# A hybrid delta-rule layer: projections ranked last, operations moved between in-order queues, and the sample states' product in 64 scaled copies on ScalarE

## Chip, cores, metric

The kernel runs on one core of a Trainium2 chip. The metric is the device time of one execution in microseconds (us): the median of several runs, and for the reading of where the time lies one profiled execution. The engines of the core are PE (matmuls; its weight loads are listed apart as PEld), DVE (VectorE), ACT (ScalarE), POOL (GpSimd) and SP (which here only issues transfers). Each works through its own instructions in order.

## What is computed

One layer of a decoder for a prompt of 1024 tokens and for eight samples of one token each, all in float32, with 1024 model columns, 8 delta heads of 128 and a feed-forward width of 2816:

```python
h = _rmsnorm(x, lp['norm1_w']) * (1 + sc1) + sh1
qkv, gdn_gate, beta_raw, a_raw, sq, sk, sv, ga, gb = _split_in(h @ lp['w_in'])
...
if st is None:
    o_a, S = _gdn_chunked(q, k, v, beta, g)              # prompt: chunks of 64
else:
    o_a, S = _gdn_recurrent(q, k, v, beta, g, st['gdn_S'])   # samples: one step
y_a = _gdn_out(o_a, gdn_gate, lp['gdn_onorm_w']) @ lp['w_gdn_out']
y_b = o_b @ lp['w_swa_out']                              # o_b: sliding-window attention with sinks
mix = (jax.nn.sigmoid(ga) * y_a + jax.nn.sigmoid(gb) * y_b) @ lp['w_o']
x = x + gt1 * mix
h2 = _rmsnorm(x, lp['norm2_w']) * (1 + sc2) + sh2
gate = h2 @ lp['w_ffn_gate']
up = h2 @ lp['w_ffn_up']
gc = _causal_dwconv(gate_ext, lp['ffn_conv_w'], L) + lp['ffn_conv_b']    # 3 taps
x = x + gt2 * ((jax.nn.silu(gc) * up) @ lp['w_ffn_down'])
```

The state of a sample's head is updated as `S = S * exp(g) + k ⊗ delta`, a 128x128 matrix for each of 64 pairs of sample and head; it is an output.

## The kernel before

Every product is made of three matmuls (L178, L179, L180 in `mm3`): both operands are split into a high part (`hi`, a ScalarE copy with rounding, L127) and the rest (`lo`, a VectorE subtraction, L128), and hi·hi, lo·hi and hi·lo are added in PSUM. So each weight tile takes a load on SP's queue (`raw`), a split on ScalarE and one on VectorE before PE can use it. Where a tile has one buffer, the next load waits for the split of the last, and the split waits for the last matmul that reads the one before.

The work goes by stages. By the times of the profile below they are: setup, modulation and attention (0 to 437 us), the delta heads (437 to 1153), the branches' output projections (1153 to 1330), the projection with w_o and the second norm (1330 to 1436), the FFN's gate and up products (1436 to 1886), its down product (to 2086) and the last chain of it with the final norm (to 2134.5).

The order of instructions on each engine is fixed when the program is built, by a scheduler that simulates the timeline and takes, among what could go next, what has the lowest priority number. `weave` sets these numbers for several streams of a delta head: each has a start and a step, and its operations get start, start + step, and so on. `unit_inverse` (start 0, step 1) inverts a head's triangular blocks: transposes and small products on PE (L1028, L1034, L1046, L1051, L1060, L1064), each followed by copies on ScalarE (L1030, L1048, L1053, L1055, L1061) or VectorE (L1035, L1057), with two rounds through DRAM on SP's queue: blocks are stored and reloaded in another layout (L987 and L992; L1015 and L1018). `delta_scan` (100, 1) walks the head's chunks (L937 to L966), `delta_prepare` makes the next head's operands, and `head_projections` the products with w_in for the head after next. `pieces` are the fillers: the products for the branch gates (`gates`, which ends in a tanh on ScalarE, L1284, an operation on GpSimd, L1285, and a store on SP, L1286) and for part of w_swa_out (`early_out`, L1306 and L1310); they start at 10000. The fillers' weights have one buffer until the head before the last.

`branches` multiplies the two branches by w_swa_out and w_gdn_out and gates them; `gate_part` loads the stored gates (L1376). Between its products `sample_delta` updates the samples' states: for each head the delta rows are loaded spread over all partitions (L1204, two buffers), GpSimd multiplies the 128x1024 tile by the keys (L1205), and VectorE adds it to the decayed state in eight operations (L1207).

`ffn_gate_up` makes the convolution in three VectorE operations per tile, of which the first (L1662) scales and adds the bias. `pair_weights` makes sums and differences of weight tiles (L1572) for a form with fewer products; they are on GpSimd except for the first tile, which is given to VectorE. `ffn_down` runs 77 steps of three matmuls on eight PSUM banks; `fetch` loads, adds and splits a step's operands some 13 steps ahead, and `take` (L1766) copies the banks out on ScalarE at the end of a chain.

## Time and profile before

| | |
|---|---|
| Time | 2136.81 us median of 3 runs (2132.54 to 2142.25) |
| Profiled execution | 2136.28 us, span 2134.5 us |
| Mean granted TensorE clock | 0.979 |
| PE busy | 2046.5 us (96%) |
| DVE, ACT, POOL busy | 1393.5 us (65%), 854.7 us (40%), 534.6 us (25%) |

A row of the stage table gives the stretch in us, its length, then busy time and (count) for PE, PEld, DVE, ACT and POOL, the mean granted clock of TensorE, the share of time that the DMA engines were busy, and GB/s. A row of a table of waits names the waiting engine, tile and line, what ended the wait, and total, times and longest in us. A row of the timeline gives start, duration, engine and operation, and in brackets the idle time ahead of it and what ended it. A row of a table of groups ends in busy us and mean ns of one, and the idle time ahead of the group. A row that gives three numbers with slashes has the minimum, median and maximum ns of one operation. "DMA b1l<-dlr: 23.1, 6" below such a row says that the engine was idle ahead of it for 23.1 us, six times, until that transfer; a row that begins with POOL there is read in the same way.

### The profile page before, as it was taken

The page shows a single profiled execution, that of the slowest core. Times are in us where ns is not written, and L with a number is a line of the kernel's source. Part 1 is how long each engine was busy: PE and PEld are TensorE (multiplying, and loading weights), DVE is VectorE, ACT ScalarE, POOL GpSimd, SP SyncE. Part 2 cuts the span into 40 slices and gives each one's busy share as a digit, 9 for nine tenths or more (in the row PEclk, how much of TensorE's full clock was granted, in tenths as well). Part 3 has the DMA queues.
Part 4 walks back from the last instruction along what each step waited for, and adds up shares of the span by engine and source line. Part 5 has one row for each costly group of instructions (what it writes and reads, how often), then busy time and mean ns, then how long its engine had stood idle before and what let it go on. Part 6 is the DMA issues. An engine that isn't in the chain of part 4 may idle for free. (4 is left out here: it accounts for less than half of the span.)

```text
span 2134.5 us, 41210 instructions
## 1 busy us (share of the span) xinstructions
PE 2046.5 (96%) x16245; PEld 1935.3 (91%) x16245; DVE 1393.5 (65%) x2781; ACT 854.7 (40%) x2125; POOL 534.6 (25%) x592
## 2 busy tenths in 40 slices
PE   7999999999899999999989989998999999999898
PEld 4985888899899999999879989898999999999898
DVE  4756667465655736557445575479888788678866
ACT  3655445434244233443343222344343343343443
POOL 1000000020221211212110220003546546545531
PEclk8999999999999999999989999999999999999999
DMA  7256442141332322313166663622333333388972
GB/s 272 86 133 204 141 161 90 49 135 48 76 85 58 83 58 54 89 52 76 48 183 211 213 224 100 182 61 71 109 95 95 110 95 95 120 285 276 317 228 85
DMA packets 301821, 274.95 MB, mean 129 GB/s; under 512 B 59666, under 2 KB 248303, under 8 KB 301612
## 3 DMA queue, kind: packets, MB, share of 16 engines
q1 hardware_dynamic: 296140, 252.49, 38.6%
q0 software_dynamic: 5200, 19.32, 2.6%
q8 instruction: 127, 2.08, 0.4%
q14 instruction: 66, 0.54, 0.1%
q10 hardware_dynamic: 288, 0.52, 0.1%
HBM read 212.54 MB, written 62.12 MB: 129 GB/s over the span
## 5 line engine op out<-in xcount | busy, mean ns | idle before, releaser
L178 PE MATMUL mm<-b1h,wh 128*128 128x384 f32 (+1 forms) x1520 | 499.0, 329 | 5.9 <-ACT gt L1284 4.1
L180 PE MATMUL mm<-b1h,wl 128*128 128x384 f32 (+1 forms) x1520 | 491.4, 325 | 2.1 <-DVE wl L128 2.1
L179 PE MATMUL mm<-b1l,wh 128*128 128x384 f32 (+1 forms) x1520 | 490.8, 323 | 0.0
L178 PEld LDWEIGHTS mm<-b1h,wh 128*128 128x128 f32 x1520 | 287.8, 190 | 15.7 <-ACT gt L1284 6.2
L180 PEld LDWEIGHTS mm<-b1h,wl 128*128 128x128 f32 x1520 | 287.3, 189 | 7.9 <-issue 4.3
L179 PEld LDWEIGHTS mm<-b1l,wh 128*128 128x128 f32 x1520 | 288.0, 189 | 3.8 <-issue 3.5
L127 ACT ACTIVATE wh<-raw 128x1024 fp32r<-128x1024 f32 x83 | 87.0, 1048 | 135.7 <-PE mm L179 75.9
L128 DVE TENSOR_TENSOR wl<-raw,wh 128x1024 fp32r<-128x1024 f32 x82 | 100.8, 1229 | 48.8 <-ACT wh L127 47.9
L179 PE MATMUL mm<-pk,w 128*128 128x260 f32 (+1 forms) x440 | 124.3, 283 | 1.1 <-DVE pk L128 1.1
L178 PE MATMUL mm<-pk,w 128*128 128x260 f32 (+1 forms) x440 | 124.3, 283 | 0.0
L180 PE MATMUL mm<-pk,w 128*128 128x260 f32 (+1 forms) x440 | 124.2, 282 | 0.0
L128 DVE TENSOR_TENSOR w<-ws,w 128x512 fp32r<-128x512 f32 x88 | 74.1, 843 | 37.4 <-ACT w L127 37.4
L1609 ACT COPY bml<-mm 128x256 f32<-128x256 f32 (+1 forms) x132 | 49.2, 374 | 108.5 <-PE mm L180 101.8
L178 PE MATMUL mm<-bmh,w 128*128 128x260 f32 (+1 forms) x320 | 90.4, 283 | 0.9 <-DVE fa L1686 0.9
L180 PE MATMUL mm<-bmh,w 128*128 128x260 f32 (+1 forms) x320 | 90.3, 282 | 0.0
L180 PE MATMUL mm<-b2h,wl 128*128 128x384 f32 (+1 forms) x256 | 83.4, 329 | 4.5 <-DVE wl L128 4.5
L178 PE MATMUL mm<-b2h,wh 128*128 128x384 f32 (+1 forms) x256 | 83.8, 329 | 2.4 <-DVE t L1327 2.4
L179 PE MATMUL mm<-b2l,wh 128*128 128x384 f32 (+1 forms) x256 | 83.9, 328 | 0.4 <-DVE b2l L128 0.4
L179 PEld LDWEIGHTS mm<-pk,w 128*128 128x128 f32 x440 | 82.8, 188 | 1.3 <-DVE pk L128 1.3
L178 PEld LDWEIGHTS mm<-pk,w 128*128 128x128 f32 x440 | 82.8, 188 | 0.3 <-ACT bml L1609 0.2
L180 PEld LDWEIGHTS mm<-pk,w 128*128 128x128 f32 x440 | 83.0, 189 | 0.0
L127 ACT ACTIVATE w<-ws 128x512 fp32r<-128x512 f32 x88 | 55.4, 632 | 49.9 <-PE wv L180 45.0
(648 smaller groups left out, 5984.1 us busy)
## 6 DMA issues: line engine op xcount, KB each, us to landing
raw<-in_w_in_dram SPq DMA_DIRECT2D x60, 512.0 KB
ws<-in_w_ffn_down_dram SPq DMA_DIRECT2D x55, 256.0 KB
raw<-xd SPq DMA_DIRECT2D x47, 258.0 KB
raw<-in_w_ffn_down_dram SPq DMA_DIRECT2D x47, 256.0 KB
raw<-in_w_ffn_gate_dram SPq DMA_DIRECT2D x22, 512.0 KB
raw<-in_w_ffn_up_dram SPq DMA_DIRECT2D x22, 512.0 KB
qst<-in_w_mod_dram SPq DMA_DIRECT2D x16, 512.0 KB
raw<-in_w_mod_dram SPq DMA_DIRECT2D x16, 512.0 KB
```

Of the source, the lines that this page charges most:

```text
L127: self.nc.scalar.activation(hi, x, AF.Copy)
L128: (eng or self.nc.vector).tensor_tensor(lo, x, hi.bitcast(F32), op=ALU.subtract)
L178: mm(ps, whi, xhi, start=first, stop=False, **kw)
L179: mm(ps, whi, xlo, start=False, stop=False, **kw)
L180: self.last_mm = mm(ps, wlo, xhi, start=False, stop=last, **kw).ins
L1609: self.last_copy = nc.scalar.copy(r[p, i], x[p])
```

## The change

Eight edits. In `weave`, the streams whose operations set the priority at which the next call begins are now those with step 1, not those with a start under 10000; the streams of projections start at 100000, behind the fillers at 10000. In `sample_delta`, ScalarE multiplies by the keys, in eight copies of 128x128 per head (L1206 of the changed kernel), in place of GpSimd. `early_out` loads part 0 of the attention's output in its fourth step. The gates that `gate_part` loads into the extra pool go through GpSimd's queue. The first tap of the FFN convolution is on ScalarE. In `ffn_down`, the splits of later steps may not be ordered ahead of the last `take`, and the last two steps of a chain fetch nothing. The second half's `ffn_states` starts at 460, the first gate weights' sums go to GpSimd, and the PSUM banks of the branches begin with another one.

```diff
@@ -1202,8 +1202,8 @@
                 yield
             d = db[:, h % 2 * NP:h % 2 * NP + NP].rearrange("p (b v) -> p b v", b=NS)
             nc.sync.dma_start(d, dlr[h].unsqueeze(0).broadcast_to([P, NS, P]))
-            nc.gpsimd.tensor_tensor(d, d, bc(kq[:, h, :, 0], 2, P), op=ALU.mult)
             for b in range(NS):
+                nc.scalar.activation(d[:, b, :], d[:, b, :], AF.Copy, scale=kq[:, h, b, 0:1])
                 nc.vector.scalar_tensor_tensor(S0[h][:, b, :], S0[h][:, b, :], self.egb[:, b, 0, h:h + 1], d[:, b, :],
                                                op0=ALU.mult, op1=ALU.add)
             nc.gpsimd.dma_start(self.O[3][0][:, h].rearrange("b k v -> k b v"), S0[h])
@@ -1252,11 +1252,11 @@
         for gen, start, step in streams:
             at = tc.cur_priority = p + start
             for _ in gen:
-                if start < 10000:
+                if step == 1:
                     end = max(end, tc.cur_priority)
                 at += step
                 tc.cur_priority = max(at, tc.cur_priority) if step == 1 else at
-            if start < 10000:
+            if step == 1:
                 end = max(end, tc.cur_priority)
         tc.cur_priority = end
 
@@ -1300,7 +1300,6 @@
         self.S0, states = [], [self.flat_room(self.b1, "b1", x, 1) for x in "hl"]
         X = {2: self.load_part(self.b1, self.ob, 2, "b1")}
         w = load(0)
-        self.obX = {0: self.load_part(self.b1, self.ob, 0, "b1")}
         for j in range(8):
             s = self.t(self.gt[0], [P, 384], self.gt[1])[:, :n]
             nc.sync.dma_start(s, self.sgb[j][:, lo:lo + n])
@@ -1309,6 +1308,8 @@
                 nc.vector.tensor_tensor(s, ps, s, op=ALU.mult)
                 nc.sync.dma_start(self.ubd[j], s)
 
+            if j == 3:
+                self.obX = {0: self.load_part(self.b1, self.ob, 0, "b1")}
             now, w = w, load(j + 1) if j < 7 else None
             if j < 6:
                 self.load_state(j, states[j // 3])
@@ -1373,7 +1374,7 @@
 
     def gate_part(self, pool, src, t):
         s = (self.t(pool, [P, 384], "gt") if pool is self.gt[0] else self.t(pool, [P, 384], "sgx", bufs=2))[:, :PARTS[t][1]]
-        self.nc.sync.dma_start(s, src)
+        (self.nc.sync if pool is self.gt[0] else self.nc.gpsimd).dma_start(s, src)
         return s
 
 
@@ -1659,7 +1660,7 @@
             e = min(c + n, NP)
             zi, ai = z[i], a[i]
             col = lambda j: fcw[:, j, f + i:f + i + 1]
-            nc.vector.tensor_scalar(ai[:, c:e], zi[:, 2 + c:2 + e], col(2), col(3), op0=ALU.mult, op1=ALU.add)
+            nc.scalar.activation(ai[:, c:e], zi[:, 2 + c:2 + e], AF.Identity, scale=col(2), bias=col(3))
             for j in (0, 1):
                 nc.vector.scalar_tensor_tensor(ai[:, c:e], zi[:, j + c:j + e], col(j), ai[:, c:e],
                                                op0=ALU.mult, op1=ALU.add)
@@ -1719,6 +1720,7 @@
                 1: ((0, 0, 1), (1, 1, 1)), 2: ((0, 1, 1), (1, 1, -1)), 6: ((1, 1, 1),)}
         steps = [(i, g) for c in chains for i in c for g in range(G)]
         ready, waiting = {}, ([], [])
+        self.took = None
         less = []
 
         def fetch(s):
@@ -1739,9 +1741,8 @@
             room = self.room(tags[s % len(tags)], [P, KC * QW])
             hi, lo = room[:, :n + 512], room[:, n + 512:2 * (n + 512)]
             with ExitStack() as after:
-                if 5 <= s < len(tags):
-                    for ins in (self.last_up, self.last_copy):
-                        after.enter_context(self.tc.issue_after(ins.ins))
+                for ins in (self.last_up, self.last_copy) if 5 <= s < len(tags) else (self.took,) if s >= len(tags) and self.took else ():
+                    after.enter_context(self.tc.issue_after(ins.ins))
                 self.split(hi, lo, raw)
             ready[s] = hi, lo
             if s == 5:
@@ -1763,20 +1764,26 @@
         def take(ps, i, p, j):
             self.turn = (self.turn + 1) % KC
             r = self.copies[:, self.turn, :256 + 4 * p]
-            nc.scalar.copy(r, ps)
+            self.took = nc.scalar.copy(r, ps)
             for k, h in enumerate(home[i]):
                 waiting[k].append((r, p, j, *h))
 
         banks = [(self.pmm, "mm", 2), (psum, "wv", 2), (psum, "wy", 2)] * 2 + [(self.pmf, "mm", 1), (psum, "nr", 1)]
         order = [(p, j) for j in range(4) for p in range(2)]
         s = done = 0
+
+        def fetch_to(n):
+            nonlocal done
+            while done < min(n, len(steps)):
+                fetch(done)
+                done += 1
+
         for c in chains[:-1]:
             ps = {(p, j): self.t(pl, [P, 512], tag, bufs=k)[:, :256 + 4 * p] for (p, j), (pl, tag, k) in zip(order, banks)}
             for i in c:
                 for g in range(G):
-                    while done < min(s + len(tags), len(steps)):
-                        fetch(done)
-                        done += 1
+                    if i != c[-1] or g < G - 2:
+                        fetch_to(s + len(tags))
                     for p, j in order:
                         step(s, ps[p, j], p, j, g == 0 and i == c[0], g == G - 1, {"skip_group_check": True} if i != c[0] else {})
                         if g == G - 1:
@@ -1788,9 +1795,7 @@
                     s += 1
         for x in waiting[0] + waiting[1]:
             add(*x)
-        while done < len(steps):
-            fetch(done)
-            done += 1
+        fetch_to(len(steps))
         self.ffn_rows(pool, psum)
         tail = self.norm_rows(pool, psum, [2 * P, 3 * P])
         chunks = [[0], [P], [], [], [4 * P, 5 * P], [6 * P, 7 * P, NP], [], []]
@@ -1892,13 +1897,13 @@
                     self.squares, self.X, self.wo = {}, {}, []
                     norm = lambda q: self.second_norm(xr, psum, q)
                     self.weave((chain(*(self.output_pass(xr, q) for q in range(4))), 0, 1),
-                               (self.ffn_states(xr, psum), 300, 30),
+                               (self.ffn_states(xr, psum), 460, 30),
                                (chain(norm(0), self.operands(xr, 0, 0)), 250, 10),
                                (chain(norm(1), self.operands(xr, 0, 1)), 490, 20),
                                (chain(norm(2), self.operands(xr, 1, 0)), 730, 120))
                 with S() as left:
                     pool = self.pool("pf", 1, ctx=left)
-                    w = self.pair_weights(pool, self.I["w_ffn_gate"][0], 0, nc.vector)
+                    w = self.pair_weights(pool, self.I["w_ffn_gate"][0], 0)
                     last, ops = norm(3), self.operands(xr, 1, 1)
                     self.weave((chain(islice(last, 3), islice(ops, 1), last, ops), -100, 1))
                     right.close()
@@ -1971,12 +1976,12 @@
                     streams = [(self.unit_inverse(pool, psum, h, prep[0]), 0, 1),
                                (self.delta_scan(pool, psum, h, prep), 100, 1)]
                     if h + 2 < H:
-                        streams[1:1] = [(chain(self.pieces(2), self.head_projections(pa, pool, h)), 500, 100)]
+                        streams[1:1] = [(chain(self.pieces(2), self.head_projections(pa, pool, h)), 100000, 100)]
                         streams.append((self.pieces(3), 10000, 100))
                     else:
                         if h + 2 == H:
-                            streams[1:1] = [(chain(self.pieces(3), *(self.delta_gate(pa, pool, i) for i in (h, h + 1))), 500, 1)]
-                        streams.append((self.head_projections(pa, pool, h), 600, 100))
+                            streams[1:1] = [(chain(self.pieces(3), *(self.delta_gate(pa, pool, i) for i in (h, h + 1))), 100000, 100)]
+                        streams.append((self.head_projections(pa, pool, h), 100000, 100))
                     if h + 1 < H:
                         streams.append((self.delta_prepare(pool, psum, h + 1), 250, 1))
                     self.weave(*streams)
@@ -1988,7 +1993,7 @@
             pool2, pool = self.pool("p6b", 1, ctx=c), self.pool("p6", 1, ctx=c)
 
             self.psm, more = self.pool("qs", 2, PSUM, ctx=c), self.pool("qb", 2, PSUM, ctx=c)
-            mm, self.mm = self.mm, [self.pmm, self.pmm, self.pmf, more, more]
+            mm, self.mm, self.turn = self.mm, [self.pmm, self.pmm, self.pmf, more, more], -1
             self.branches(pool, pool2)
             self.mm = mm
         cg.close()
```

How this moves instructions is seen at three places. The first is ScalarE around the last head's inverse (tmp_12089 and w_1927 are its copies, b1h are the high parts of the attention's output for `early_out`, loaded just before, gt the fillers' tanh). Before:

```order
L127 ACTIVATE b1h_1987_12296<-b1l_1988_12297 128x528 x2
L127 ACTIVATE b1h_1992_12316<-b1l_1993_12317 128x768
L127 ACTIVATE wh_12406<-raw_12404 128x1024
L1284 ACTIVATE gt_11818<-mm_11793 128x384
L127 ACTIVATE b1h_1992_12316<-b1l_1993_12317 128x768
L1048 COPY tmp_12089<-tp_12088 32x256 x2
L127 ACTIVATE b1h_1992_12316<-b1l_1993_12317 128x768 x2
L1053 COPY w_1927_12125<-tp_12090 32x256
```

After:

```order
L942 ACTIVATE s_11504<-rc_11502,c_1722_10850 128x128
L1284 ACTIVATE gt_11696<-mm_11671 128x384
L1048 COPY tmp_12089<-tp_12088 32x256 x2
L942 ACTIVATE s_11518<-rc_11516,c_1722_10850 128x128
L1039 COPY W_4463<-T_12005 32x8x32 x4
L959 ACTIVATE osq_1846_11526,so_11400<-o_11463 128x128
L1053 COPY w_1927_12125<-tp_12090 32x256
L1055 COPY W_4463<-tp_12090 32x8x32 x2
L959 ACTIVATE osq_1846_11526,so_11400<-o_11463 128x128
L127 ACTIVATE wh_12312<-raw_12310 128x1024
```

The inverse's copies now come ahead of all splits of the attention's output. On PE at the same place, before (mm_12339 is a filler's product, tp the inverse's):

```order
L1046 MATMUL tp_12088<-MR_12010,U_1902_11947 32x32 x16
L178 MATMUL mm_12339<-b1h_1987_12296,wh_12312 128x264
L179 MATMUL mm_12339<-b1l_1988_12297,wh_12312 128x264
L180 MATMUL mm_12339<-b1h_1987_12296,wl_12313 128x264
L1051 MATMUL tp_12090<-T_12005,tmp_12089 32x32 x16
L1060 MATMUL tp_12130<-MR_12010,UZ_11948 64x64 x8
L1064 MATMUL tp_12140<-W_4463,UZ_11948 64x64 x8
```

After, the beginning of the same piece:

```order
L1046 MATMUL tp_12088<-MR_12010,U_1902_11947 32x32 x16
L940 MATMUL rc_11516<-y_11512,W_4463 128x128
L178 MATMUL mm_11700<-b1h_14_152,wh_11638 128x264
L179 MATMUL mm_11700<-b1l_15_153,wh_11638 128x264
L180 MATMUL mm_11700<-b1h_14_152,wl_11639 128x264
L178 MATMUL mm_11700<-b1h_14_152,wh_11638 128x264
L179 MATMUL mm_11700<-b1l_15_153,wh_11638 128x264
L180 MATMUL mm_11700<-b1h_14_152,wl_11639 128x264
L1051 MATMUL tp_12090<-T_12005,tmp_12089 32x32 x15
```

Six matmuls of a gate filler instead of three of `early_out` stand between L1046 and L1051; behind L1051, where L1060 and L1064 followed at once, 29 matmuls of fillers now stand ahead of L1060 and 24 ahead of L1064.

The second place is ScalarE in the branches (b1l_2049 is the tile with the delta rows, kq the keys, raw_134xx and raw_136xx weights of w_gdn_out, b2l the normed delta output). Before:

```order
L127 ACTIVATE b2h_2110_13382<-osm 128x8x8
L127 ACTIVATE wh_13178<-raw_13176 128x1024
L127 ACTIVATE b2h_2110_13382<-b2l_2111_13383 128x2x256 x4
L127 ACTIVATE wh_13426<-raw_13424 128x1024
L127 ACTIVATE b2h_2112_13398<-b2l_2113_13399 128x768 x4
L127 ACTIVATE wh_13432<-raw_13430 128x1024
L127 ACTIVATE wh_13636<-raw_13634 128x1024
```

After:

```order
L127 ACTIVATE b2h_2110_13438<-osm 128x8x8
L1206 ACTIVATE b1l_2049_12696<-b1l_2049_12696,kq 128x128 x6
L127 ACTIVATE wh_13178<-raw_13176 128x1024
L1206 ACTIVATE b1l_2049_12696<-b1l_2049_12696,kq 128x128 x2
L127 ACTIVATE b2h_2110_13438<-b2l_2111_13439 128x2x256 x4
L1206 ACTIVATE b1l_2049_12696<-b1l_2049_12696,kq 128x128 x8
L127 ACTIVATE wh_13482<-raw_13480 128x1024
L1206 ACTIVATE b1l_2049_12696<-b1l_2049_12696,kq 128x128 x16
L127 ACTIVATE b2h_2112_13454<-b2l_2113_13455 128x768 x4
L127 ACTIVATE wh_13488<-raw_13486 128x1024
L1206 ACTIVATE b1l_2049_12696<-b1l_2049_12696,kq 128x128 x24
L127 ACTIVATE wh_13692<-raw_13690 128x1024
```

The weights' splits, which were ahead of everything but the branch's own operands, now have 8 to 24 copies ahead of them. (The first eight copies stand one row above this piece.)

The third place is SP's queue early in the delta heads (T and wd are the inverse's tiles, gt a filler's finished gate, raw a weight tile of w_in: 5438, 6160 and 6256 for projections, 6124 for a filler). Before:

```order
L1015 DMA wd_152_943<-T_4881 32x8x16 x4
L133 DMA raw_5438<-in_w_in_dram 128x8x128
L1018 DMA T_4942<-wd_152_943 32x8x32 x4
L133 DMA raw_6160<-in_w_in_dram 128x8x128
L133 DMA raw_6256<-in_w_in_dram 128x8x128
```

After:

```order
L1015 DMA wd_152_943<-T_4881 32x8x16 x4
L1286 DMA sgb_3914<-gt_5699 128x264
L133 DMA raw_6124<-in_w_in_dram 128x8x128
L1018 DMA T_4942<-wd_152_943 32x8x32 x4
L133 DMA raw_5438<-in_w_in_dram 128x8x128
L1286 DMA sgb_3914<-gt_5734 128x384
```

A filler's store and its next weight load now stand between the inverse's store and its reload, and the projection's load has gone behind.

## Prediction

> **What bounds the kernel now.** I read the stage table first, then each stage's table of waits, then the timeline around the worst of them. The stage table (busy time of each engine in eight stretches: setup and attention, delta heads, branches, output projection, FFN start, gate/up, down, tail; PEclk is the granted clock):
>
> ```profile
> 0.00:437.00 437.00, 410.82 (x2570) 330.92 (x2570) 258.38 (x687) 215.96 (x657) 23.06 (x61) 0.96 0.44 142
> 437.00:1153.00 716.00, 690.39 (x6112) 667.78 (x6113) 417.09 (x887) 267.25 (x779) 132.20 (x188) 0.98 0.31 83
> 1153.00:1330.00 177.00, 167.83 (x1107) 164.37 (x1105) 106.92 (x238) 43.99 (x89) 25.60 (x19) 0.98 0.60 188
> 1330.00:1436.00 106.00, 100.87 (x826) 99.63 (x827) 65.52 (x123) 44.10 (x78) 2.73 (x5) 0.98 0.44 131
> 1436.00:1500.00 64.00, 57.77 (x469) 55.76 (x468) 54.80 (x83) 27.16 (x53) 25.73 (x24) 1.00 0.24 73
> 1500.00:1886.00 386.00, 385.85 (x3237) 385.54 (x3236) 310.37 (x508) 157.17 (x315) 215.83 (x222) 1.00 0.35 109
> 1886.00:2086.00 200.00, 193.14 (x1599) 192.30 (x1599) 152.86 (x173) 84.45 (x113) 104.83 (x67) 0.98 0.80 275
> 2086.00:2134.50 48.50, 39.83 (x338) 39.04 (x336) 27.60 (x86) 14.61 (x48) 4.59 (x8) 0.93 0.24 91
> sum 2134.50, PE 2046.50 PEld 1935.34 DVE 1393.54 ACT 854.69 POOL 534.57; mean PE 255.81 PEld 241.92 DVE 174.19 ACT 106.84 POOL 66.82
> ```
>
> The first number is the stretch's length, the second PE's busy time. PE is the bound: it is idle for 88 us of 2134.5, and the number of matmuls stays the same. Nothing can be won but idle PE time and time at a lower granted clock. By length less busy, the delta heads hold 25.6 us of idle PE, the branches 9.2, the projection 5.1, the FFN start 6.2, down 6.9, and gate/up 0.15. The first 437 us hold 26.2 more, but there the change does nothing. So whatever is taken off VectorE in gate/up is worth nothing. Who PE waits for, in the delta heads, then in the branches, then down:
>
> ```profile
> PE tp L1051 <- ACT tmp L1048: 4.1, 1, 4.1
> PE mm L178 <- ACT gt L1284: 4.1, 7, 1.3
> PE tp L1064 <- ACT W L1055: 3.2, 2, 1.6
> PE tp L1060 <- DVE MR L1057: 2.8, 1, 2.8
> PE mm L180 <- DVE wl L128: 2.1, 2, 1.4
> ...
> PE mm L180 <- DVE wl L128: 4.5, 2, 2.7
> PE mm L178 <- DVE t L1327: 2.4, 1, 2.4
> PE mm L179 <- DVE b2l L128: 0.4, 1, 0.4
> ...
> PE mm L178 <- ACT bml L1766: 6.8, 3, 5.0
> ```
>
> (Microseconds in total, times, the longest.) The list is short: one bad place in the last head's inverse, some weight changes of the gate fillers, two gaps in the branches, one in down. Each has a shadow in the clock; these windows of 50 us show it:
>
> ```profile
> 1100.00:1150.00 50.00, 41.01 (x364) 39.19 (x363) 24.57 (x43) 20.33 (x45) 3.84 (x5) 0.86 0.74 217
> 1200.00:1250.00 50.00, 44.54 (x243) 43.10 (x242) 32.82 (x71) 10.40 (x13) 19.83 (x13) 0.93 0.84 284
> 1950.00:2000.00 50.00, 45.02 (x363) 44.81 (x362) 42.95 (x53) 21.96 (x29) 26.92 (x19) 0.93 0.81 272
> ```
>
> A granted mean of 0.93 over 50 us is 7 us at half clock, 0.86 is 14 us; matmuls in that time lose half of it.
>
> **The weave (projections ranked last).** Here are PE's waits in the last head's inverse, then ScalarE's row at the same time:
>
> ```profile
> 1108.00 1.45 PE L1051 MATMUL tp<-T,tmp 32*32 32x32 f32 x32 [4.15 <-ACT tmp L1048]
> 1112.19 1.94 PE L1060 MATMUL tp<-MR,UZ 64*64 64x64 f32 x16 [2.75 <-DVE MR L1057]
> 1114.80 1.96 PE L1064 MATMUL tp<-W,UZ 64*64 64x64 f32 x16 [0.67 <-ACT UZ L1061]
> 1117.43 0.80 PE L940 MATMUL rc<-vn,W 128*128 128x128 f32 x2 [0.67 <-ACT W L1065]
> ...
> 1104.66 0.84 ACT L127 ACTIVATE b1h<-b1l 128x768 fp32r<-128x768 f32 x1 [2.70 <-DMA b1l<-ob]
> ...
> 1106.72 0.83 ACT L127 ACTIVATE b1h<-b1l 128x768 fp32r<-128x768 f32 x1
> 1107.58 0.75 ACT L1048 COPY tmp<-tp 32x256 f32<-32x256 f32 x2
> ```
>
> The copy L1048 takes 0.75 us, but it stands behind splits of the next stage's operands, and the first of these waits 2.70 us for a load. PE has three matmuls to do meanwhile. In the changed order the copy stands ahead of these splits, and the gate fillers, no longer eaten up early by the projections' rank, lie between the steps: six matmuls ahead of L1051, 29 ahead of L1060, 24 ahead of L1064. The four waits are 4.15 + 2.75 + 0.67 + 0.67 = 8.2 us; of the 14 us at half clock 8.2 are idle anyway, so the other 6 us cost 3. At most 11 us; I take 8, since six matmuls don't quite cover 0.75 us of copies and the fillers used here are missing behind. Low end 3: only the ScalarE queue clears.
>
> The fillers keep one set of weights, so a change of weights needs other work beside it. The changed order alternates filler and projection, and the filler's weight changes without cover become about half as many: of 4.1 + 2.1 us I take 2 (0 to 4). Against it, some steps of other heads' inverses lose cover: I take +1, from 0 to +5 (nearest row, the two L1064 waits of 1.6 us each, three more of which are 4.8). Together **−9, from −15 to +2.**
>
> **Sample states.** The rows, over the whole run, of GpSimd's product, VectorE's update behind it, and ScalarE's nearest operations (minimum/median/maximum ns), and VectorE's waits at the update:
>
> ```profile
> L1205 POOL TENSOR_TENSOR b1l<-b1l,kq x8: 1895/1902/3342, 1211.5 to 1255.8; 128x1024 f32<-128x1024 f32 x8
>   DMA b1l<-dlr: 23.1, 6
>   POOL b1l L1205: 9.2, 4
> L942 ACT ACTIVATE s<-rc,c x64: 348/368/378, 523.7 to 1144.8; 128x128 f32<-128x128 f32 x64
> L127 ACT ACTIVATE bmh<-t 128x128 fp32r<-128x128 f32 x16 | 4.8, 301 | 18.3 <-DVE t L1332 18.3
> 1230.23 0.69 PE L180 MATMUL mm<-b2h,wl 128*128 128x384 f32 x1 [2.75 <-DVE wl L128]
> 1237.97 0.41 PE L178 MATMUL mm<-b2h,wh 128*128 128x384 f32 x1 [2.35 <-DVE t L1327]
> ```
>
> VectorE stood 9.2 us behind L1205, and the weights' low part (wl) and the gated product (t), for which PE waited 2.75 and 2.35 us, stood behind that on VectorE. Now 64 ScalarE copies of 128x128 replace eight operations of 1.9 us or more. No such copy is in the trace: L942 (scaled, from PSUM) gives 64 × 0.368 = 23.6 us, L127 at 128x128 gives 19.3. I take L942's form, the only one with a scale by column, as the ceiling, and 20 us. ScalarE was busy for 10.4 of the 50 us from 1200, so it fits; but it serves in order, and eight groups, each with its own load of the state rows (GpSimd waited 23.1 us in six of them), stand ahead of weight splits. [...]
>
> Saved are 2.75 + 2.35 + 0.36 = 5.5 us of waits, and the 7 us at half clock (3.5 lost): at most 9. The second wait for wl (1.74, the rest of the 4.5) stays, as the split it needs is now behind 24 copies. I take **−6, from −9 to +3** (+3: a head's load, 23.1 / 6 = 3.9 us, is once waited for by a split that PE needs, with the old gaps half gone).
>
> [...]
>
> **FFN convolution's first tap.** VectorE's row in 1440 to 1500, and ScalarE's nearest:
>
> ```profile
> L1662 DVE TENSOR_SCALAR fa<-fz,fcw 128x512 f32<-128x512 f32 x4 | 2.1, 537 | 0.0
> L1671 ACT ACTIVATE fz<-fa x44: 622/637/644, 1469.6 to 1881.2; 128x512 f32<-128x512 f32 x22, 128x520 f32<-128x520 f32 x22
> ```
>
> All 44 are 24 us off VectorE and 44 × 0.637 = 28 us onto ScalarE (157 busy of 386: room). Only the four in 1440 to 1500, where VectorE is full and PE waits, count: 2.1 us earlier at best, **−1.5, from −2 to +1.**
>
> **Edits at nothing.** The first gate weights' sums move to GpSimd: VectorE there waited for their load with dg behind it, and PE for dg:
>
> ```profile
> L1572 DVE TENSOR_TENSOR ws<-raw,raw 128x512 f32<-128x512 f32 x1 | 0.7, 693 | 6.8 <-DMA raw<-in_w_ffn_gate_dram 6.8
> PE nr L1489 <- DVE dg L1488: 2.8, 1, 2.8
> ```
>
> But dg needs GpSimd's power, which now stands behind the same three sums; the block changes its queue: 0, from −2 to +2. The gate loads on GpSimd's queue clear SP for the output weights, but their split stays behind the last operand splits on ScalarE: −0.5. The states' later start leaves PE's order as it is. In down, the splits held behind the copies (took) change their order around the 5.0 us wait by one place only, and the split that blocks there waits for a load: 0, from −4 (wait and shadow gone) to +4. The last split of down now stands behind VectorE's sixteen sums, but PE takes its low part 46 matmuls later, so its lateness is covered: 0, to +1.
>
> **The sum.** −9 − 6 − 1.5 − 0.5 = −17. On the profiled execution, 2136.28 us (span 2134.5 and 1.8 around it), that is 2119.3; the median of before, 2136.81, is 0.5 above it, so **2120**. With the terms' ends combined as independent (6, 4, 1.5, 4) the forecast's own range is 2111 to 2128.
>
> **Rivals.** *Given back:* fillers are a fixed stock. If the 24-matmul blocks at the last inverse are missing at the second to sixth head, each gets a wait like L1064's 1.6 with as much lost to the clock: five times 2.4 = 12, the delta heads end at +3 and the sum at −5: about 2132. For it: the total of PE work is unchanged and covers get thinner in several places. Against it: heads two to six had covers of over 2 us to give.
>
> *Slower: SP's queue.* SP issues in order, and waits for the gates it stores:
>
> ```profile
> SPq L1286 <- POOL gt L1285: 187.6, 35, 17.5
> ```
>
> That is 5.4 us each. The new order puts such a store and a weight load between the inverse's own store (L1015) and reload (L1018). Where the filler isn't done by then, the reload, the inverse and the scan behind it come late. It decides from the point where the delay exceeds the cover, some 2 to 3 us: in six heads 6 × 5.4 = 32, and with −17 the time is about 2152. Against it: in the first such place the filler's matmuls are placed well ahead of the reload.
>
> *The change does not bite:* in the branches ScalarE's queue passes VectorE's wait on to the weights' splits, and the last inverse's copies wait for another load: −2, about 2135.
>
> **Chances.** 0.55 forecast, 0.05 more gain than that (the clock in other windows), 0.18 given back, 0.09 does not bite, 0.13 slower. A measurement of this kernel tells about 0.5% (10.7 us) from no change. Faster by more: the forecast's and more, 0.60; slower by more: 0.13; between: 0.27. The range 2107 to 2141 leaves out the slower case and some of the largest gain.
>
> **What would show it.** Right: no wait at L1051 and L1060 above 1 us, clock of the last inverse's window above 0.95; VectorE not waiting at L1207 for more than 3 us; ScalarE some 20 us busier around 1230; gate/up still without idle PE. Wrong: new waits of PE in heads one to six adding up to over 5 us; SP waiting in L1286 ahead of L1018; PE waiting for a wh split behind L1206.

## The result, and the profile after

The changed kernel takes 2116.18 us (median of 6 runs, 2111.08 to 2119.43) against 2134.27 us before (6 runs): a ratio of 0.9907, interval 0.9887 to 0.9927, 18 us less. The profiled execution's span is 2115.1 us.

The page of the changed kernel, busy time:

```profile
PE 2043.1 (97%) x16245; PEld 1929.3 (91%) x16245; DVE 1358.1 (64%) x2733; ACT 902.8 (43%) x2233; POOL 519.9 (25%) x594
```

PE's idle time went from 88 to 72 us. To see where, the stages are measured between the start times of the same instructions in each trace, since the program has moved as a whole (worked out from the traces; us):

| From … to | before | changed | weave alone | copies alone | tap alone |
|---|---|---|---|---|---|
| start … first L1028 (code unchanged) | 494.0 | 495.5 | 492.8 | 492.3 | 494.1 |
| … last L944 (delta heads) | 651.4 | 640.9 | 642.0 | 654.2 | 650.8 |
| … first product with w_o (branches) | 184.7 | 179.8 | 185.7 | 179.1 | 185.2 |
| … last product of a norm with dg | 115.7 | 114.8 | 109.8 | 112.9 | 113.7 |
| … first copy out of down (FFN) | 471.7 | 466.5 | 470.9 | 473.7 | 466.8 |
| … last copy out of down | 169.5 | 169.1 | 168.4 | 167.7 | 170.2 |
| … end | 47.5 | 48.5 | 47.8 | 48.6 | 47.5 |

The first row is the same code in all five, and differs by up to 3 us: that is the scatter against which a single profile is read. Delta heads −10.5, branches −4.9, FFN −5.3, and little elsewhere. Of the FFN's 5.3 us, 0.7 is only that the first copy out of down stood behind a split on ScalarE before.

The branches' figure is that of one profile. In eight profiles of kernels with all the edits of that stage (the changed kernel twice, and six profiles of the kernels below that are built on it) it took 178.3 to 184.3 us, and in four without the copies 184.7 to 186.5. The delta heads are steadier: 640.5 to 642.5 us in the same eight.

PE's waits in the changed kernel's delta heads, then in its branches, the projection and down:

```profile
PE rc L944 <- ACT s L942: 3.9, 6, 1.2
PE tp L1064 <- ACT W L1055: 3.2, 2, 1.6
PE rc L940 <- DVE y L938: 2.9, 5, 1.1
PE mm L178 <- ACT gt L1284: 2.0, 5, 0.6
...
PE mm L178 <- ACT wh L127: 2.4, 2, 1.4
PE mm L1423 <- ACT w L127: 2.1, 1, 2.1
PE mm L179 <- DVE b2l L128: 1.1, 2, 0.6
PE mm L180 <- DVE wl L128: 0.8, 1, 0.8
...
PE nr L1490 <- DVE dg L1489: 2.6, 1, 2.6
...
PE mm L178 <- ACT bml L1767: 5.0, 2, 4.4
```

L1051 and L1060 are gone from the list. There are two L1064 waits of 1.6 us as before, but not at the same heads: before they stood at the fourth and the seventh, now at the sixth and the seventh. The sixth head's is this one:

```profile
943.43 1.14 PE L1064 MATMUL tp<-W,UZ 64*64 64x64 f32 x16 [1.61 <-ACT W L1055]
```

With three smaller waits beside it, it makes 3.2 us, and the clock granted from 940 to 960 us is 0.83, where it was 1.00 before. Waits for filler weights (wl, gt) fell from 6.2 us to 2.0. The scan's waits (L944, L940) have grown from 3.4 to 6.8 us; before they were

```profile
PE rc L940 <- DVE y L938: 1.8, 2, 1.1
PE rc L944 <- ACT s L942: 1.6, 4, 0.6
```

The windows of 50 us around the worst places, the last of them from the place where the last inverse now stands:

```profile
1200.00:1250.00 50.00, 46.69 (x276) 45.20 (x276) 37.97 (x100) 30.05 (x82) 7.16 (x8) 1.00 0.88 300
900.00:950.00 50.00, 46.76 (x477) 43.57 (x476) 29.11 (x48) 20.75 (x65) 4.81 (x8) 0.95 0.15 38
1000.00:1050.00 50.00, 44.98 (x479) 42.29 (x478) 24.10 (x52) 19.98 (x68) 6.20 (x7) 0.93 0.21 61
1100.00:1150.00 50.00, 45.22 (x336) 43.05 (x335) 28.41 (x51) 21.07 (x45) 7.45 (x10) 1.00 0.92 268
1050.00:1100.00 50.00, 49.09 (x512) 46.30 (x511) 23.15 (x66) 15.60 (x45) 11.10 (x17) 1.00 0.30 72
```

The windows at 1100 and 1200, 0.86 and 0.93 before, are granted 1.00, and so is the one at 1050, which counts here because the last inverse now begins at 1086 us instead of 1103. In the branches this does not hold in every profile: the same kernel profiled again (the first of the three side by side below) was granted 0.97 from 1200 to 1250 us, with

```profile
PE mm L178 <- ACT wh L127: 4.7, 2, 3.7
```

where the table above has 2.4 us and 1.4 as the longest. That wait is for a weight of w_gdn_out whose split on ScalarE in its turn waits for the load: in the changed kernel SP issued it at 1220.4 us and the split began at 1231.6, after ScalarE had stood idle for it for 0.95 us (2.05 us in the second profile). Here is the last inverse in the timeline of PE, and then of ScalarE:

```profile
1086.41 0.69 PE L1046 MATMUL tp<-MR,U 32*32 32x32 f32 x32
1088.18 0.69 PE L1051 MATMUL tp<-T,tmp 32*32 32x32 f32 x30
```

```profile
1087.20 0.75 ACT L1048 COPY tmp<-tp 32x256 f32<-32x256 f32 x2 [1.68 <-PE tp L1046]
```

ScalarE now stands idle ahead of the copy, waiting for PE; before it was the other way round.

### The profile page after: what moved, and what is told of

It is laid out like the page before. It is cut to its first block, busy times and chain, and to the rows that moved or that the text cites. A ratio compares the mean times of both kernels' runs of the same rounds, so it can differ in the third digit from the quotient of the medians.

```text
span 2115.1 us, 41340 instructions
## 1 busy us (share of the span) xinstructions
PE 2043.1 (97%) x16245; PEld 1929.3 (91%) x16245; DVE 1358.1 (64%) x2733; ACT 902.8 (43%) x2233; POOL 519.9 (25%) x594
## 4 chain that ended last, share of the span: by engine, by line
PE 76%; DVE 6%; DMA 6%; issue 5%; ACT 2%; POOL 1%; SPq 1%; DVEq 0%; POOLq 0%; ACTq 0%
PE mm L178 16%; PE mm L180 16%; PE mm L179 16%; PE wv L178 2%; PE wv L180 2%; PE wv L179 2%; PE wy L178 1%; PE wy L180 1%; PE wy L179 1%; PE mm L262 1%; PE pv L645 1%; PE tp L188 1%; PE pv L643 1%; PE sc L606 1%; PE pt L188 1%
## 5 line engine op out<-in xcount | busy, mean ns | idle before, releaser
L128 DVE TENSOR_TENSOR wl<-raw,wh 128x1024 fp32r<-128x1024 f32 x82 | 100.2, 1223 | 55.6 <-ACT wh L127 54.0
L128 DVE TENSOR_TENSOR w<-ws,w 128x512 fp32r<-128x512 f32 x88 | 77.5, 881 | 37.1 <-ACT w L127 36.9
L1665 DVE SCALAR_TENSOR_TENSOR fa<-fz,fcw,fa 128x512 f32<-128x512 f32 x88 | 73.5, 854 | 18.4 <-ACT fa L1663 18.1
```

The source lines that it names most:

```text
L128: (eng or self.nc.vector).tensor_tensor(lo, x, hi.bitcast(F32), op=ALU.subtract)
L1665: nc.vector.scalar_tensor_tensor(ai[:, c:e], zi[:, j + c:j + e], col(j), ai[:, c:e], op0=ALU.mult, op1=ALU.add)
```

## The experiments

**The weave alone**, on the kernel before:

```diff
-                if start < 10000:
+                if step == 1:
...
-   ... self.head_projections(pa, pool, h)), 500, 100)]
+   ... self.head_projections(pa, pool, h)), 100000, 100)]
```

> The kernel before with the change to the weave alone (priority of the next call from streams with step 1; projections at 100000). Theory: this gives the whole gain of the delta heads, as its order on ScalarE and PE at the last head's inverse is that of the full change: waits at L1051, L1060 and L1064 of that head from 8.2 us to under 1, waits for filler weights from about 5 us to under 1, the end of the delta scan about 10 us earlier, the whole time 9 to 12 us shorter than before; branches, FFN and down as before. Rival (the later load of the attention's output is needed too): the 2.7 us wait of ScalarE for that load still stands ahead of L1048, half of the 8.2 us stays, and the gain is 4 to 6 us.

2120.61 us against 2136.31 on that chip, ratio 0.9917 (0.9894 to 0.9940): 15.7 us less. The delta heads went to 642.0 us, within 1.1 of the full change: the weave gives all of that stage, and the later load of the attention's output isn't needed for it. But the whole gain is larger than the 9 to 12 us expected. The rest is in the projection's stage, 109.8 us instead of 115.7, where nothing was changed. The experiments on that stage return to it.

**The queue or the cover?** The weave changes two things at the last inverse, ScalarE's order and the matmuls between PE's steps. This kernel changes only the first: the operand splits of the attention's output go to GpSimd, and PE's order there stays.

```diff
-        self.nc.scalar.activation(hi, x, AF.Copy)
+        if hi_eng is not None:       # GpSimd, for load_part(..., "b1")
+            hi_eng.tensor_scalar(hi, x, 1.0, None, op0=ALU.mult)
+        else:
+            self.nc.scalar.activation(hi, x, AF.Copy)
```

> The kernel before, with the high parts of the attention's output for early_out and the first branch part (b1h, eight operations) made by GpSimd instead of ScalarE. PE's order at the last head's inverse stays that of before (three matmuls ahead of L1051, none ahead of L1060 and L1064), only ScalarE's queue ahead of the copy L1048 is cleared of these splits (its lines are two higher here). Queue theory (the splits waiting for their load made the 4.15 and half of the 2.75 us): the first wait falls to about 1 us, the second to about 1.5, the two of 0.67 stay, 8.2 us become about 4, and the clock of that window rises above 0.90. Cover theory (the missing matmuls made it): the four waits stay above 6.5 us in sum.

2127.16 us, ratio 0.9949 (0.9930 to 0.9967). PE at the last inverse (lines are two higher), and its window:

```profile
1103.95 1.08 PE L1053 MATMUL tp<-T,tmp 32*32 32x32 f32 x32 [0.56 <-ACT tmp L1050]
1107.36 1.94 PE L1062 MATMUL tp<-MR,UZ 64*64 64x64 f32 x16 [2.33 <-DVE MR L1059]
1109.96 1.96 PE L1066 MATMUL tp<-W,UZ 64*64 64x64 f32 x16 [0.67 <-ACT UZ L1063]
1112.60 0.80 PE L942 MATMUL rc<-vn,W 128*128 128x128 f32 x2 [0.67 <-ACT W L1067]
```

```profile
1100.00:1150.00 50.00, 43.76 (x387) 42.00 (x385) 28.73 (x47) 16.09 (x39) 18.10 (x14) 0.90 0.76 225
```

8.2 us became 4.2, as the queue theory had it, though not in its parts: the first wait lost 3.6 us, the second only 0.4. So half of the last inverse's waits were the queue; the other half goes only with the weave, which puts matmuls between the steps. The stage itself ended only 2.8 us earlier, near the scatter, and 5.0 us of this kernel's gain were again in the projection (110.6 us).

**The copies alone:**

```diff
-            nc.gpsimd.tensor_tensor(d, d, bc(kq[:, h, :, 0], 2, P), op=ALU.mult)
             for b in range(NS):
+                nc.scalar.activation(d[:, b, :], d[:, b, :], AF.Copy, scale=kq[:, h, b, 0:1])
```

> The kernel before with the sample states' product as 64 copies on ScalarE alone. Theory: VectorE no longer waits at L1207 nor shares time with GpSimd, PE's waits of 2.75 and 2.35 us near 1230 and 1238 shrink to about 2 us in sum, the clock of 1200 to 1250 goes from 0.93 to 1.00, and the branches are 4 to 6 us shorter; the copies take about 0.3 to 0.37 us each. Rival (the branches gained by the other bank order and the gates' queue): the branches' time stays within 1.5 us of before.

2130.61 us, ratio 0.9969 (0.9955 to 0.9984). The branches are 179.1 us instead of 184.7: all of the stage's gain, so the other bank order and the gates' queue are not needed for it. One part of the theory fell. The copies in this kernel, and then the updates (L1207) with what VectorE waited for ahead of them:

```profile
L1206 ACT ACTIVATE b1l<-b1l,kq x64: 385/387/403, 1213.9 to 1252.8; 128x128 f32<-128x128 f32 x64
```

```profile
L1207 DVE SCALAR_TENSOR_TENSOR b1h<-b1h,egb,b1l x40: 340/347/353, 1214.4 to 1253.9; 128x128 f32<-128x128 f32 x40
...
  ACT b1l L1206: 7.0, 4
```

VectorE still waits there for 7.0 us (8.8 in the full change, 9.2 before); ScalarE now waits 13.7 us for the same loads, where GpSimd waited 23.1. What differs is what stands behind the waits. VectorE before, with GpSimd's product of the same time, then VectorE in this kernel:

```profile
1224.71 3.87 DVE L1207 SCALAR_TENSOR_TENSOR b1h<-b1h,egb,b1l 128x128 f32<-128x128 f32 x8 [1.33 <-POOL b1l L1205]
1228.50 0.55 DVE L1327 TENSOR_TENSOR t<-mm,gt 128x384 f32<-128x384 f32 x1
1228.97 1.21 DVE L128 TENSOR_TENSOR wl<-raw,wh 128x1024 fp32r<-128x1024 f32 x1
1226.01 1.90 POOL L1205 TENSOR_TENSOR b1l<-b1l,kq 128x1024 f32<-128x1024 f32 x1 [0.46 <-DMA gt<-sgb]
```

```profile
1223.81 1.40 DVE L1207 SCALAR_TENSOR_TENSOR b1h<-b1h,egb,b1l 128x128 f32<-128x128 f32 x5
1225.13 0.55 DVE L1327 TENSOR_TENSOR t<-mm,gt 128x384 f32<-128x384 f32 x1
1225.60 0.87 DVE L1207 SCALAR_TENSOR_TENSOR b1h<-b1h,egb,b1l 128x128 f32<-128x128 f32 x3
1226.38 1.22 DVE L128 TENSOR_TENSOR wl<-raw,wh 128x1024 fp32r<-128x1024 f32 x1
```

An update needs only its own copy of 0.39 us, not the whole product, the gated product is ordered between updates, and no group takes 3.87 us for eight as it did beside GpSimd (2.27 here). Before, three of the 64 updates took 2.0 us instead of 0.34; each began within 0.1 us of the start of a product on GpSimd and ended within 0.2 us of its end. Here the longest takes 0.35 us. The weight's split comes 2.6 us earlier, in a trace in which the branches began 1.2 us later, and PE's 2.75 us wait for it is gone.

**The tap alone:**

```diff
-            nc.vector.tensor_scalar(ai[:, c:e], zi[:, 2 + c:2 + e], col(2), col(3), op0=ALU.mult, op1=ALU.add)
+            nc.scalar.activation(ai[:, c:e], zi[:, 2 + c:2 + e], AF.Identity, scale=col(2), bias=col(3))
```

> The kernel before with the first tap of the FFN convolution on ScalarE alone. In the full change the stretch from the second norm to the first copy out of down became 5.3 us shorter, of which the prediction had 1.5. Theory: the tap alone gives it, PE's waits around 1484 to 1495 (3.7 us before) fall to under 1 and the time is 3 to 5 us shorter. Rival (the gate weights' sums on GpSimd and the down product's splits give it): the time is within 1.5 us of before.

2132.84 us, ratio 0.9980 (0.9965 to 0.9995). The FFN stretch is 466.8 us instead of 471.7, as in the full change (466.5). Before, PE waited there for VectorE's work on the convolution:

```profile
PE wv L178 <- DVE bml L1684: 3.0, 2, 1.6
PE mm L178 <- DVE fa L1686: 0.7, 1, 0.7
```

In this kernel PE's waits from 1440 to 1500 are

```profile
PE wv L178 <- ACT w L127: 1.1, 1, 1.1
PE mm L179 <- DVE pk L128: 1.1, 1, 1.1
PE wv L179 <- DVE pk L128: 0.3, 1, 0.3
```

and those three (1.6, 0.7 and 1.4 us) are gone. Over the whole FFN the taps cost ScalarE more than the nearest row said:

```profile
L1663 ACT ACTIVATE fa<-fz,fcw 128x512 f32<-128x512 f32 x44 | 35.7, 814 | 3.9 <-DVE fz L1653 3.4
```

(the changed kernel, 1430 to 1900), and PE has no idle time in 1500 to 1886 all the same.

**The projection's stage.** Three parts alone gave 15.7 + 5.7 + 3.5 = 25 us, the whole change 18. The intervals of the parts reach 5, 3 and 3 us to either side and that of the whole 4, so by time alone no loss is shown. The table points to one between the first product with w_o and the last norm, where the parts alone gained 5.8, 2.7 and 2.0 us and the whole 0.9. PE's largest wait there is that for dg, 2.8 us before and 2.6 after. In the kernel with the weave alone it was under 0.2 us. The chain ahead of dg in the changed kernel, in the timeline of VectorE and then of GpSimd:

```profile
1346.56 0.16 DVE L1485 TENSOR_SCALAR rs<-nr 128x2 f32<-128x2 f32 x1 [0.65 <-PE nr L1480]
1354.56 0.42 DVE L1489 TENSOR_TENSOR dg<-ident,rs 128x256 f32<-128x256 f32 x1 [4.91 <-POOL rs L123]
```

```profile
1349.97 1.28 POOL L1573 TENSOR_TENSOR ws<-raw,raw 128x512 f32<-128x512 f32 x1 [39.32 <-DMA raw<-in_w_ffn_gate_dram]
1351.34 1.29 POOL L1573 TENSOR_TENSOR ws<-ws,raw 128x512 f32<-128x512 f32 x1
1352.58 1.26 POOL L1573 TENSOR_TENSOR ws<-raw 128x512 f32<-128x512 f32 x1
1353.80 0.72 POOL L123 TENSOR_TENSOR rs<-rs,mhalf 128x2 f32<-128x2 f32 x1
```

rs was ready at 1346.7, and the power that it needs (L123) ran at 1353.8, behind three sums that waited for a load. So I gave the sums back to VectorE in one kernel, and in another kept them on GpSimd but ordered them behind the first norm's power.

```diff
-                    w = self.pair_weights(pool, self.I["w_ffn_gate"][0], 0)
+                    w = self.pair_weights(pool, self.I["w_ffn_gate"][0], 0, nc.vector)
```

> The changed kernel with the first gate weights' sums given back to VectorE. The prediction put this edit at nothing, since the block only changes its queue. Theory: it is near nothing, but not because the queues are equal: on GpSimd three sums of 1.3 us stand ahead of the power that dg needs, on VectorE three of 0.69 us; so PE's wait for dg falls from 2.6 us by up to 1.7 us, and the time by 1 to 3 us with the clock. Rival (the block is the load's landing alone): the wait stays within 0.5 us and the time within 1 us of the changed kernel.

2117.30 us, ratio 0.9910 (0.9893 to 0.9927). My theory was wrong here: dg's wait is 3.7 us, not shorter, and the stage 116.3 us. On VectorE the sums are quick, but rs itself stands behind them there. Its rows on VectorE:

```profile
1350.41 0.69 DVE L1573 TENSOR_TENSOR ws<-raw,raw 128x512 f32<-128x512 f32 x1 [7.89 <-DMA raw<-in_w_ffn_gate_dram]
1352.74 0.15 DVE L1485 TENSOR_SCALAR rs<-nr 128x2 f32<-128x2 f32 x1
```

On either engine it is the load's landing (1350.4, against 1350.0) that decides, as the rival's mechanism had it, though the wait changed by 1.1 us, more than the 0.5 that it allowed.

```diff
-        self.power(rs[:, :nc_], rs[:, :nc_], self.mhalf)
+        root = self.power(rs[:, :nc_], rs[:, :nc_], self.mhalf)
+        self.root = self.root or root
...
-            (eng or self.nc.gpsimd).tensor_tensor(s, x, y, op=op)
+            with self.tc.issue_after(self.root.ins) if f == 0 else nullcontext():
+                (eng or self.nc.gpsimd).tensor_tensor(s, x, y, op=op)
```

> The changed kernel with the first gate weights' sums on GpSimd as there, but ordered behind the first norm's power. Theory: nothing that waits for the load stands ahead of dg any more; PE's wait for dg (2.6 us) goes, the granted clock of the 20 us around it goes from about 0.9 to 1.00, and the time falls by 3 to 5 us against the changed kernel, to about 2112. Rival (dg waits for VectorE's own work): the wait stays above 2 us and the time is that of the changed kernel.

2112.86 us, ratio 0.9899 (0.9881 to 0.9916). GpSimd's timeline in this kernel, then windows of 20 us around dg, here and in the changed kernel:

```profile
1344.18 0.73 POOL L123 TENSOR_TENSOR rs<-rs,mhalf 128x2 f32<-128x2 f32 x1 [36.67 <-ACT nss L1403]
1346.57 1.28 POOL L1575 TENSOR_TENSOR ws<-raw,raw 128x512 f32<-128x512 f32 x1 [1.67 <-PE mm L180]
```

```profile
1342.00:1362.00 20.00, 20.00 (x171) 19.95 (x171) 10.62 (x19) 8.54 (x17) 4.64 (x4) 1.00 0.37 122
```

```profile
1346.00:1366.00 20.00, 17.36 (x132) 16.98 (x132) 8.02 (x16) 7.97 (x16) 4.47 (x4) 0.91 0.28 95
```

The wait for dg is gone, the window's clock is 1.00 instead of 0.91, and the stage is 110.8 us, 4.0 less.

**The first weight of w_o by GpSimd**, added to that:

```diff
+            if j == 0:
+                self.nc.gpsimd.tensor_scalar(w[0][:, c], raw[:, c], 1.0, None, op0=ALU.mult)
+                self.nc.vector.tensor_tensor(w[1][:, c], raw[:, c], w[0][:, c].bitcast(F32), op=ALU.subtract)
+            else:
+                self.split(*(x[:, c] for x in w), raw[:, c])
```

> As the run before, and the high part of the first output weight tile is made by GpSimd, which is idle there, instead of ScalarE. Theory: PE's wait of 2.06 us at the first product with w_o comes from that split standing behind the branches' last operand splits on ScalarE; it falls below 0.8 us and the time by 2 to 4 us more (with the clock of 0.83 in the 10 us behind it), to about 2109. Rival (the wait is for the operand's own last split, whatever the weight does): the wait stays and the time is that of the run before.

2115.56 us, ratio 0.9907 (0.9893 to 0.9922): no gain. The wait at L1423 is gone, and these came in its place:

```profile
PE mm L178 <- ACT pk L127: 3.0, 3, 1.5
PE mm L180 <- DVE pk L128: 1.5, 2, 0.8
```

PE begins earlier and then waits for the splits of the next weight tiles, which still go through ScalarE and VectorE. The stage took 113.6 us, against 110.8 in the kernel that it was added to.

**Without the edit in down:**

```diff
-                for ins in (self.last_up, self.last_copy) if 5 <= s < len(tags) else (self.took,) if s >= len(tags) and self.took else ():
+                for ins in (self.last_up, self.last_copy) if 5 <= s < len(tags) else ():
...
-                    if i != c[-1] or g < G - 2:
-                        fetch_to(s + len(tags))
+                    fetch_to(s + len(tags))
```

> The changed kernel without the edit in the down product (splits held behind the copies, no fetch in a chain's last two steps). The prediction put it at 0, from -4 to +4. Theory: the wait of 4.4 us for the copies stays at 4 to 5 us and the time is within 2 us of the changed kernel. Rival: the edit is what took 0.8 us off the waits of down, and without it down is 1 to 3 us longer.

2112.29 us, ratio 0.9903 (0.9884 to 0.9921), and down took 169.3 us, as with the edit (169.1). The large wait for the copies is 4.1 us. The edit is worth nothing that can be measured; whether its lower median was real is the question of the last kernel below.

**On one chip, side by side:** the changed kernel, the kernel with the power first, and that kernel without the edit in down.

> The changed kernel again, as the measure for the two others on the same chip: about 17 to 20 us below before.

> The kernel with the first norm's power ahead of the gate weights' sums, again, beside the changed kernel. Theory: dg's wait and its clock are worth about 4 us, so it is 3 to 5 us below the changed kernel on this chip. Rival (its 3 us lower median was the scatter of the setup, whose length varies by up to 3 us between runs of the same code): within 1 us of it.

> The power ahead of the sums, and the down product's edit taken back. Theory: the edit in down is worth nothing, so this is within 1.5 us of the run before it. Rival (its lower median without the edit in down was real): 2 to 4 us below it.

Against 2134.78 before: 2115.54 us (0.9907, 0.9890 to 0.9924), 2112.95 us (0.9897, 0.9877 to 0.9917) and 2113.62 us (0.9897, 0.9877 to 0.9917). Side by side the power ahead of the sums gave 2.6 us, and 3.3 by the medians of the earlier, separate sets of runs; the intervals overlap, so by time alone it isn't separated from the changed kernel. By the trace it is: the projection's stage was 114.8, 114.8, 116.3 and 115.0 us in four profiles with a load-bound sum ahead of the power or of rs, and 110.8, 110.1 and 110.0 us in the three with the power first and the weights of w_o as they were. Taking back the edit in down changed nothing.

## Why the prediction was right

The forecast was −17 us to 2120, with 2107 to 2141; −18.1 us to 2116.2 came. By the stages of the one profile the gain is 21 us, while the start, whose code is the same, took 1.5 us longer. The two large terms came out much as reasoned; that the total lies so near is in part luck, since the FFN gave 3.8 us more than its term and the branches 1.1 less. Term by term:

- *Delta heads, −9 (−15 to +2): −10.5.* The mechanism was as written, the queue and the cover at the last inverse. Its 8.2 us went altogether, where I took 8 with the clock; six matmuls and the scan's own products do cover 0.75 us of copies. The ceiling of 11 us was a little low: the clock fell to 0.50 only at 1106.8 us, so 5.4 and not 8.2 of those 14 us were idle, and the rest cost some 4 us instead of 3. The filler weights gave 4.2 us where I took 2. Against that stand new waits: in the scan's own chain at the end, 3.4 us more at L940 and L944, and 3.2 us around the sixth head's inverse, while the fourth head's wait of 1.6 us is gone. The +1 of that term was mis-sized.
- *Branches, −6 (−9 to +3): −4.9, or −5.6 alone.* The clock of the window rose to 1.00 as said, though to 0.97 in the second profile of the same kernel. The sign that I gave, VectorE not waiting over 3 us at L1207, did not show: it waits 8.8 us, and the gain comes from where the waits lie. A sign of being wrong did show, PE waiting for a wh split on ScalarE, for 1.4 us here and 3.7 in the second profile; but that split waited last for its weight's load, not for the copies ahead of it. One copy took 0.387 us, above the ceiling of 0.368 that I drew from L942; since eight in a row take 2.45 us, all 64 kept ScalarE busy for 19.6 us, the 20 that I took. The window's clock was 0.93 before, with gaps of 2.75 and 2.35 us and 6.8 us at a clock of 0.50, and 1.00 in the changed kernel, where the longest gap was 1.4 us. In nine profiles of kernels with these copies the three whose longest wait there was under 1.5 us kept full clock, and the six with 1.8 to 3.7 us had 3.4 or 6.8 us at a clock of 0.50. A short gap wasn't always free, though: around the sixth head's inverse the clock fell to 0.83 over 20 us with none above 1.61.
- *FFN, −1.5 (−2 to +1): −5.3.* This is the term that was mis-sized. I bounded it by the time of four taps on VectorE, 2.1 us; but three waits of PE for that convolution (3.7 us) went altogether with the tap alone, and all but 0.7 us of them in the whole change. On what else VectorE got faster there the runs don't decide: some of its operations were longer in that stretch before, as the eight splits of raw weights (L128, 128x512), with 1.00 us on average against 0.71 with the tap alone and in the whole change.
- *The sums on GpSimd, at nothing: right in size.* The block did change its queue, as said, and given back to VectorE the sums made dg no earlier (3.7 us of wait). What I didn't see is that on either engine the sums make dg depend on a load. After the first product with w_o it landed 34.1 us before, 33.7 in the changed kernel and 33.9 with the sums given back; in the weave alone it landed after 32.0 us, and dg came in time. Why the load came sooner there stays open, and it isn't the whole of it: with the tap alone it landed after 32.2 us and PE still waited 2.5 us for dg. With the power ahead of the sums the load no longer matters to dg, and 4 us of the stage are won that the change leaves lying.
- *w_o's loads −0.5, down 0, tail 0:* the 2.1 us wait for the first split stays, down is −0.4, the tail +1.0, all within the scatter.

The rivals: *given back* came true at one of its five heads, the sixth, which got a wait of 1.6 us with lost clock, as that rival described; the wait of the same size at the fourth head is gone, so there was little to pay in sum. *SP's queue* did not bite: SP waited 179.7 us for stores of gates (187.8 before in the same stretch), and no wait of PE is put down to a reload of the inverse.

## What to carry to other kernels

Look for the short operation that stands behind a load's consumer in an in-order queue; here reordering it was worth its wait of 2.6 us and the lower clock behind it, 4 us of the stage, and it is found by reading two engines at the same time stamp. A move to another engine doesn't help when the moved work waits for the same load and the new queue holds an operation on the critical chain: order it behind that operation instead. Test parts alone, and set them against the whole by stages: their sum (25 us against 18) was within the noise, but the stage table pointed to the place where 4 us could still be won. And profile the same kernel again before a gain of a few us in one stage is believed.

## What the runs showed of the hardware

On ScalarE 128x512 with a scale and a bias by column took 816 ns here, against 637 for L1671, a tanh without them at 512 and 520 columns, and 128x128 with one scale 387 ns. In the kernel before, 32 products of 32x32 took 0.69 us at a granted clock of 1.00 (L1046) and 1.45 us at 0.50 (L1051). The setup, whose code is the same in all, took 492.2 to 495.5 us from profile to profile.
